# A tiled 4096 x 4096 x 4096 matmul with bias and tanh: the opening's loads of B moved to SyncE as float32, A put first on GpSimd's queue, the first phase cut from eight k-tiles to six, and transposes moved ahead of adds

## The chip, the cores and the metric

The kernel runs on one core of a Trainium2 chip. The metric is the device time of one execution in microseconds (us), lower is better. Rates: 1 GB/s is 1 KB/us, and 1 MB/us is 1,000 of these. A load "lands" when its last byte has arrived.

## The reference

```python
def setup_inputs():
    m, k, n = 4096, 4096, 4096
    return {"a": randn(m, k), "b": randn(k, n), "bias": randn(n)}    # float32

def reference(a, b, bias):
    return np.tanh(np.matmul(a, b) + bias)
```

## The kernel before

The kernel multiplies in float16, with A's contraction index k on the partitions. A k-tile is a group of 128 values of k. GpSimd's loads cast from float32 to float16 on the way in; VectorE (DVE) turns A in 32 x 32 blocks. The partitions are used as four quarters of 32: partition 32q + p of k-tile t holds row 1024q + 32t + p of B. So one k-tile of B is four separate strips of 32 rows, each loaded by a DMA of its own.

The steady state (most of the run) multiplies rows of A, 128 at a time, with a 1024-column strip of B that lies in SBUF. The opening is special, because B's first strip has to arrive first. It works on two groups of four row tiles, in this order: group 0 on the first `KS` k-tiles, group 1 on the same `KS` k-tiles, then group 0 on the rest, then group 1 on the rest. The kernel has eight PSUM buffers, so partial sums are put aside in SBUF (`spill`) and added later.

```python
    KS = 8                       # k-tiles in the first phase (of KT = 32)
    AN = 3                       # buffers for untransposed A
    WARM = 24                    # matmuls on zeros, to warm the clock
    ...
    def load_b(bt, n0, t0, nt, q):               # one of four quarters, cast by GpSimd's DMA
        src = b[ds(q * KQ + t0 * QP, nt * QP), ds(n0, NCW)]
        nc.gpsimd.dma_start(out=bt[t0 // TB][ds(q * QP, QP), ds(t0 % TB, nt), :],
                            in_=src.rearrange("(t p) n -> p t n", p=QP))
    ...
    def turn(at, key, mb0, t0, nt):              # transpose on VectorE, frees A's buffer after use
        pump()                                   # issues queued loads, at most AN of A
        transpose_a(at, staged[key][0], mb0, t0, nt)
        ...
    want_a("g0a", 2, 0, 2 * Q, 0, KS)            # the queue of loads, all on GpSimd
    want(lambda: load_b_all(0, 2))
    want_a("g0b", 2, 2 * P, 2 * Q, 0, KS)
    for t in range(2, KS, 2):
        want(lambda t=t: load_b_all(t, 2))
    want(lambda: load_bias(bias_bc, 0))
    want_a("g1a", 2, 4 * P, 2 * Q, 0, KS)
    want_a("g1b", 2, 6 * P, 2 * Q, 0, KS)
    for t in range(KS, KT, TA):                  # TA = 8: then A and B for the rest
        want_a(("g0", t), G, 0, G * Q, t, TA)
        for u in range(t, t + TA, TB):
            want(lambda u=u: load_b_all(u, TB))
    for m in range(G):
        want_a(("g1", m), 1, (G + m) * P, Q, KS, KT - KS)
    ...
    def aside0(ps, m, j):                        # group 0's first sums are put aside ...
        put_aside(ps, m, j)
        if (m, j) == (1, 1):
            turn1(0)                             # ... group 1's first transpose among them
    down(ps, KS - 2, KS, aside0)
    turn1(1)
    ...
    def end0(ps, m, j):                          # group 0's last adds, tanh and stores
        end(ps, m, j)
        if (m, j) == (1, 1):
            turn2(0)                             # group 1's next transpose, behind four adds
    down(ps, KT - TB, KT, end0)
```

Of the kernel before, what the change touches and what calls it, by code (L numbers as in the profile page):

```python
# [13 lines left out]
P = 128  # L14
Q = 4
QP = 32
NB = 512
fp32 = mybir.dt.float32
# [4 lines left out]
def kernel(  # L23
# [7 lines left out]
    nc = tc.nc  # L31
# [4 lines left out]
    KQ = K // Q  # L36
    KT = K // P
    MT = M // P
    NCW = 1024
    NC = N // NCW  # L40
    J = NCW // NB
    TB = 4
    G = 4
    KS = 8
    AN = 3
    WARM = 24

    singles = ctx.enter_context(tc.tile_pool(name="singles", bufs=1))
    bpool = ctx.enter_context(tc.tile_pool(name="bpool", bufs=2))
# [2 lines left out]
    biasp = ctx.enter_context(tc.tile_pool(name="biasp", bufs=2))  # L52
# [32 lines left out]
            an[:, ds(mb0, Q), :].rearrange("P mb (t k) -> P mb t k", k=QP),  # L85
        )

    def load_bias(bias_bc, n0):
        src = bias[ds(n0, NCW)]
        nc.gpsimd.dma_start(  # L90
            out=bias_bc,
            in_=bass.AP(tensor=src.tensor, offset=src.offset, ap=[[0, P], *src.ap]),
        )


    queue, live, staged = [], [0], {}
# [9 lines left out]
    def want_a(key, uses, *where):  # L106
        queue.append((key, uses, lambda: load_a(*where)))

    def want(load):
        queue.append((None, 0, load))  # L110

    def turn(at, key, mb0, t0, nt):
        pump()
        transpose_a(at, staged[key][0], mb0, t0, nt)
        staged[key][1] -= 1
        if not staged[key][1]:
            live[0] -= 1
            pump()
# [3 lines left out]
            ps, at[:, t, :], bt[t // TB][:, t % TB, ts(j, NB)], start=start, stop=stop  # L122
        )

    def finish(ps, addend, mi, c0, w=NB, o_sb=None, pieces=1):

        if o_sb is None:
            o_sb = opool.tile([P, w], fp32, name="o_sb")
        w //= pieces
        for i in range(pieces):  # L130
            piece = ds(i * w, w)
            nc.vector.tensor_tensor(  # L132
                out=o_sb[:, piece], in0=ps[:, piece], in1=addend[:, piece], op=mybir.AluOpType.add
            )
            nc.scalar.activation(  # L135
                o_sb[:, piece], o_sb[:, piece], mybir.ActivationFunctionType.Tanh
            )
            nc.sync.dma_start(out=out[ds(mi * P, P), ds(c0 + i * w, w)], in_=o_sb[:, piece])



# [12 lines left out]
    def put_aside(ps, m, j):  # L154
        nc.vector.tensor_tensor(  # L155
            out=aside(m, j), in0=ps, in1=bias_bc[:, ts(j, NB)], op=mybir.AluOpType.add
        )

    def end(ps, m, j):
        finish(ps, aside(m, j), m, j * NB, o_sb=aside(m, j))  # L160

    def banks():
        return [[psum.tile([P, NB], fp32, name="ps") for j in range(J)] for m in range(G)]

    def load_b_all(t0, nt):
        for q in range(Q):
            load_b(b_cur, 0, t0, nt, q)

    def across(ps, ms, t0, nt, first):
        for t in range(t0, t0 + nt):  # L170
            for m in ms:
                for j in range(J):
                    mm(ps[m][j], ats[m], b_cur, t, j, t == first, False)

    def down(ps, t0, t1, done):
        for m in range(G):
            for j in range(J):
                for t in range(t0, t1):
                    mm(ps[m][j], ats[m], b_cur, t, j, False, t == t1 - 1)
                done(ps[m][j], m, j)  # L180
# [15 lines left out]
        nc.tensor.matmul(warm, zeros[:, :P], zeros, start=i == 0, stop=i == WARM - 1)  # L196


    TA = 8
    want_a("g0a", 2, 0, 2 * Q, 0, KS)  # L200
    want(lambda: load_b_all(0, 2))
    want_a("g0b", 2, 2 * P, 2 * Q, 0, KS)
    for t in range(2, KS, 2):
        want(lambda t=t: load_b_all(t, 2))
    bias_bc = biasp.tile([P, NCW], fp32, name="bias_bc")
    want(lambda: load_bias(bias_bc, 0))
    want_a("g1a", 2, 4 * P, 2 * Q, 0, KS)
    want_a("g1b", 2, 6 * P, 2 * Q, 0, KS)
    for t in range(KS, KT, TA):
        want_a(("g0", t), G, 0, G * Q, t, TA)  # L210
        for u in range(t, t + TA, TB):
            want(lambda u=u: load_b_all(u, TB))
    for m in range(G):
        want_a(("g1", m), 1, (G + m) * P, Q, KS, KT - KS)
    todo = [(c, mi) for c in range(NC) for mi in range(MT) if (c, mi) >= (0, 2 * G)]

    ps = banks()
    turn(ats[0], "g0a", 0, 0, KS)
    turn(ats[1], "g0a", Q, 0, KS)
    across(ps, (0, 1), 0, 2, 0)  # L220
    turn(ats[2], "g0b", 0, 0, KS)
    turn(ats[3], "g0b", Q, 0, KS)
    across(ps, (2, 3), 0, 2, 0)
    across(ps, range(G), 2, KS - 4, 0)

    def turn1(m):
        turn(ats[G + m], "g1a" if m < 2 else "g1b", (m % 2) * Q, 0, KS)

    def aside0(ps, m, j):
        put_aside(ps, m, j)  # L230
        if (m, j) == (1, 1):
            turn1(0)

    down(ps, KS - 2, KS, aside0)
    turn1(1)


    def turn0(t, m):
        turn(ats[m], ("g0", t), m * Q, t, TA)

    def before1(m, j):
        if m < 6 and j == 0:
            turn1(m - 2)
        if m == 6:
            turn0(KS, j)
        if m == 7:
            turn0(KS, 2 + j)

    group1(0, KS, put_aside, before1)


    ps = banks()
    for t in range(KS, KT, TA):
        if t > KS:
            for m in range(G):
                turn0(t, m)
        across(ps, range(G), t, TA - TB if t + TA == KT else TA, KS)

    def turn2(m):
        turn(ats[G + m], ("g1", m), 0, KS, KT - KS)  # L260

    def end0(ps, m, j):
        end(ps, m, j)
        if (m, j) == (1, 1):
            turn2(0)

    down(ps, KT - TB, KT, end0)


    ahead = 3  # L270
# [24 lines left out]
    for i, (c, mi) in enumerate(todo):  # L295
        if mi == 0:
            b_cur, bias_bc = b_next, bias_next
        if c + 1 < NC and mi == (2 * G if c == 0 else 0):
            b_next = new_b()
            left = [(s, q) for s in range(KT // TB) for q in range(Q)]  # L300
        if i + ahead < len(todo):
            want_row(i + ahead)
        for s, q in left[:2]:
            want(lambda s=s, q=q, c=c, bt=b_next: load_b(bt, (c + 1) * NCW, s * TB, TB, q))
        left = left[2:]
        if c + 1 < NC and mi == MT - 4:
            bias_next = biasp.tile([P, NCW], fp32, name="bias_bc")
            want(lambda c=c, bb=bias_next: load_bias(bb, (c + 1) * NCW))
        pump()
        if i + 2 < len(todo):  # L310
            new_at(i + 2)
        at = at_q.pop(0)
        for j in range(J):

            halves = 2 if i == len(todo) - 1 and j == J - 1 else 1
            w = NB // halves
            for h in range(halves):
                ps = psum.tile([P, w], fp32, name="ps")
                c0 = j * NB + h * w
                for t in range(KT):  # L320
                    nc.tensor.matmul(  # L321
                        ps,
                        at[:, t, :],
                        b_cur[t // TB][:, t % TB, ds(c0, w)],
                        start=t == 0,
                        stop=t == KT - 1,
                    )
                finish(ps, bias_bc[:, ds(c0, w)], mi, c * NCW + c0, w, pieces=halves)


# [28 lines left out]
```

## Time and profile before

| | before |
|---|---|
| time, median of the first 3 runs | 1792.26 us (1791.81 to 1792.65) |
| matmuls of the product | 8,192 of 0.2158 us = 1,768 us |
| first matmul of the product starts | 11.35 us |
| last matmul ends, span ends | 1785.5 us, 1789.8 us |
| B's k-tiles 24 to 27 land, first used | 70.8 us, 71.6 us |
| group 1's second block of A lands, its transpose starts | 79.6 us, 82.8 us |

The page of before opens with the busy time of each engine, in us, and its share of the span; its clock row has one digit for each fortieth of the span.

```profile
PE 1779.1 (99%) x8248; PEld 807.4 (45%) x8248; DVE 745.0 (42%) x420; ACT 162.7 (9%) x260; POOL 358.0 (20%) x668
...
PEclk9999999999999999999999999999999999999999
```

TensorE is busy 99% of the span at full clock, on this scale. All there is to win is in the first 90 us and the last 4, so the views below look at those. First, TensorE's waits in before: who ended them, us in total, how many, the longest.

```profile
PE ps L121 <- DMA b<-in_b_dram: 2.9, 1, 2.9
PE ps L121 <- DVE atx L83: 1.3, 2, 0.7
...
PE ps L121 <- DVE at L83: 1.0, 1, 1.0
```

The 2.9 us are the wait for B at 8.5 to 11.35 us. The 1.0 us is for the second block of A. The 1.3 us are two waits for group 1's transposes, 0.7 us near 29 us and 0.62 us near 86 us.

Next, stretches of before: us from the span's start, length, then busy us and instructions of PE, PEld, DVE, ACT and POOL, the granted clock, the DMA share and the GB/s written by DMAs.

```profile
5.00:10.00 5.00, 3.45 (x16) 1.40 (x14) 2.17 (x2) 0.00 (x0) 3.63 (x7) 1.00 1.08 143
10.00:15.00 5.00, 3.05 (x8) 0.93 (x8) 1.14 (x2) 0.00 (x0) 3.81 (x8) 0.69 1.28 195
15.00:20.00 5.00, 4.55 (x14) 1.54 (x15) 1.42 (x2) 0.00 (x0) 4.25 (x8) 0.63 1.11 197
40.00:50.00 10.00, 10.00 (x48) 4.51 (x47) 5.10 (x6) 0.00 (x0) 4.45 (x8) 1.00 1.30 202
```

The clock is the share of full speed that TensorE was granted, a mean over the stretch. It is 0.69 and 0.63 between 10 and 20 us, after TensorE had nothing to do from 8.5 to 11.35 us. The DMAs write float16, so 202 GB/s written are about 0.40 MB/us read. The first ten microseconds are far below that.

Last, the timeline of before: start, length, engine, line, operation, how many, and in brackets the idle time ahead of it and what ended that.

```profile
11.35 3.05 PE L121 MATMUL ps<-b,at 128*128 128x512 f16 x8 [2.90 <-DMA b<-in_b_dram]
...
14.05 2.37 DVE L83 STREAM_TRANSPOSE at<-an 128x1024 f16<-128x1024 f16 x2 [3.86 <-DMA an<-in_a_dram]
...
15.36 14.06 PE L121 MATMUL ps<-b,at 128*128 128x512 f16 x56 [0.95 <-DVE at L83]
...
82.80 3.37 DVE L83 STREAM_TRANSPOSE atx<-an 128x3072 f16<-128x3072 f16 x1
...
86.23 9.02 PE L121 MATMUL ps<-b,atx 128*128 128x512 f16 x41 [0.62 <-DVE atx L83]
```

The transposes for rows 2 and 3 start at 14.05 us and the matmuls that need them at 15.36. (K-tile 24's first use, 71.6 us in the table, is group 0's second phase at 44.0 us plus 128 matmuls of 0.2158 us; no wait lies between.) At 82.80 us group 1's transpose starts although its data landed at 79.6 us: it stands behind group 0's adds in VectorE's order, and TensorE waits for it until 86.23 us.

### The profile page before, as it was taken

The page shows a single profiled execution, that of the slowest core. Times are in us where ns is not written, and L with a number is a line of the kernel's source. Part 1 is how long each engine was busy: PE and PEld are TensorE (multiplying, and loading weights), DVE is VectorE, ACT ScalarE, POOL GpSimd, SP SyncE. Part 2 cuts the span into 40 slices and gives each one's busy share as a digit, 9 for nine tenths or more (in the row PEclk, how much of TensorE's full clock was granted, in tenths as well). Part 3 has the DMA queues.
Part 4 walks back from the last instruction along what each step waited for, and adds up shares of the span by engine and source line. Part 5 has one row for each costly group of instructions (what it writes and reads, how often), then busy time and mean ns, then how long its engine had stood idle before and what let it go on. Part 6 is the DMA issues. An engine that isn't in the chain of part 4 may idle for free.

```text
span 1789.8 us, 19352 instructions
## 1 busy us (share of the span) xinstructions
PE 1779.1 (99%) x8248; PEld 807.4 (45%) x8248; DVE 745.0 (42%) x420; ACT 162.7 (9%) x260; POOL 358.0 (20%) x668
## 2 busy tenths in 40 slices
PE   8999999999999999999999999999999999999999
PEld 3444444444444444444444444444444444444444
DVE  5463344334433444334433443344334433444341
ACT  0110000000000000000000000000000000000001
POOL 6422222211222211111132222111111111111100
PEclk9999999999999999999999999999999999999999
DMA  9999887665777865655588777555665555655621
GB/s 182 214 189 189 155 159 147 125 132 114 159 147 144 170 140 108 121 119 124 106 168 156 158 142 142 121 112 107 127 120 112 112 113 109 125 112 111 120 70 41
DMA packets 138630, 238.26 MB, mean 133 GB/s; under 512 B 14769, under 2 KB 27569, under 8 KB 138545
## 3 DMA queue, kind: packets, MB, share of 16 engines
q0 software_dynamic: 101248, 169.91, 56.6%
q1 hardware_dynamic: 37296, 67.13, 10.3%
q8 instruction: 64, 1.05, 0.2%
q14 instruction: 22, 0.17, 0.0%
HBM read 337.64 MB, written 67.11 MB: 226 GB/s over the span
## 4 chain that ended last, share of the span: by engine, by line
PE 95%; DMA 4%; POOL 1%; issue 1%; DVE 0%; ACT 0%; ACTq 0%; DVEq 0%; POOLq 0%
PE ps L321 92%; PE ps L121 2%; DMA b<-in_b_dram 2%; DMA an<-in_a_dram 1%; POOL b L66 0%; DMA bias_bc<-in_bias_dram 0%; POOL an L75 0%; DVE atx L83 0%; ACT o_sb L135 0%; DVE o_sb L132 0%; ACTq L354 0%; DVEq L132 0%; POOLq L343 0%
## 5 line engine op out<-in xcount | busy, mean ns | idle before, releaser
L321 PE MATMUL ps<-b,at 128*128 128x512 f16 x7712 | 1657.8, 378 | 0.0
L321 PEld LDWEIGHTS <-at 128*128 128x128 f16 x7712 | 754.6, 98 | 903.3
L132 DVE TENSOR_TENSOR o_sb<-ps,bias_bc 128x512 f32<-128x512 f32 (+1 forms) x243 | 166.4, 686 | 977.8 <-PE ps L321 764.1
L83 DVE STREAM_TRANSPOSE at<-an 128x4096 f16<-128x4096 f16 (+1 forms) x136 | 551.0, 4056 | 26.7 <-DMA an<-in_a_dram 26.7
L75 POOL DMA_DIRECT2D an<-in_a_dram x524 | 282.8, 547 | 1296.6 <-DVE at L83 1224.4
L135 ACT ACTIVATE o_sb<-o_sb 128x512 f32<-128x512 f32 (+1 forms) x243 | 151.5, 624 | 1505.7 <-DVE o_sb L132 1505.7
L66 POOL DMA_DIRECT2D b<-in_b_dram x136 | 73.2, 542 | 55.2 <-PE ps L321 28.6
L121 PE MATMUL ps<-b,at 128*128 128x512 f16 x256 | 58.6, 391 | 3.9 <-DMA b<-in_b_dram 2.9
L121 PE MATMUL ps<-b,atx 128*128 128x512 f16 x256 | 55.7, 379 | 1.3 <-DVE atx L83 1.3
L121 PEld LDWEIGHTS <-at 128*128 128x128 f16 x256 | 25.3, 100 | 37.1 <-issue 5.7
L121 PEld LDWEIGHTS <-atx 128*128 128x128 f16 x256 | 24.8, 98 | 32.2 <-DVE atx L83 2.7
L132 DVE TENSOR_TENSOR spill<-ps,spill 128x512 f32<-128x512 f32 x16 | 10.7, 684 | 25.7 <-PE ps L121 25.4
L135 ACT ACTIVATE spill<-spill 128x512 f32<-128x512 f32 x16 | 10.0, 630 | 117.2 <-DVE spill L132 117.2
L83 DVE STREAM_TRANSPOSE atx<-an 128x1024 f16<-128x1024 f16 (+1 forms) x8 | 18.3, 2295 | 0.0
L155 DVE TENSOR_TENSOR spill<-ps,bias_bc 128x512 f32<-128x512 f32 x16 | 10.1, 670 | 10.0 <-PE ps L121 10.0
L196 PE MATMUL ps<-zeros 128*128 128x512 f16 x24 | 7.3, 476 | 1.2 <-DVE zeros L193 1.2
L196 PEld LDWEIGHTS <-zeros 128*128 128x128 f16 x24 | 2.8, 118 | 5.2 <-issue 2.5
L90 POOL DMA_DIRECT2D bias_bc<-in_bias_dram x4 | 2.3, 563 | 0.1
L135 ACT ACT_TABLE_LOAD x1 | 1.3, 1283 | 0.7 <-PEq L343 0.7
L193 DVE MEMSET zeros<- 128x256 uint32 x1 | 0.3, 272 | 0.9 <-PEq L343 0.9
L343 POOL MEMSET const-float32-0.0<- 128x1 f32 x1 | 0.1, 98 | 0.2 <-issue 0.2
L343 POOL MEMSET const-bfloat16-1.0<- 128x1 bf16 x1 | 0.1, 101 | 0.0
(2 smaller groups left out, 0.2 us busy)
## 6 DMA issues: line engine op xcount, KB each, us to landing
an<-in_a_dram POOLq DMA_DIRECT2D x492, 256.0 KB, 5.4
out_dram<-o_sb SPq DMA_DIRECT2D x239, 256.0 KB, 4.3
b<-in_b_dram POOLq DMA_DIRECT2D x120, 256.0 KB, 8.9
out_dram<-spill SPq DMA_DIRECT2D x16, 256.0 KB, 6.4
an<-in_a_dram POOLq DMA_DIRECT2D x16, 192.0 KB, 7.8
an<-in_a_dram POOLq DMA_DIRECT2D x16, 128.0 KB, 5.7
b<-in_b_dram POOLq DMA_DIRECT2D x16, 128.0 KB, 5.0
bias_bc<-in_bias_dram POOLq DMA_DIRECT2D x4, 512.0 KB, 8.2
```

The source lines that it names most:

```text
L66: nc.gpsimd.dma_start(out=bt[t0 // TB][ds(q * QP, QP), ds(t0 % TB, nt), :], in_=src.rearrange("(t p) n -> p t n", p=QP),)
L75: nc.gpsimd.dma_start(out=an[ds(q * QP, QP), :, :], in_=src.rearrange("(mb p) k -> p mb k", p=QP),)
L83: nc.vector.transpose(at[:, ds(t0, nt), :].rearrange("P t (mb p) -> P mb t p", p=QP), an[:, ds(mb0, Q), :].rearrange("P mb (t k) -> P mb t ...
L90: nc.gpsimd.dma_start(out=bias_bc, in_=bass.AP(tensor=src.tensor, offset=src.offset, ap=[[0, P], *src.ap]),)
L121: nc.tensor.matmul(ps, at[:, t, :], bt[t // TB][:, t % TB, ts(j, NB)], start=start, stop=stop)
L132: nc.vector.tensor_tensor(out=o_sb[:, piece], in0=ps[:, piece], in1=addend[:, piece], op=mybir.AluOpType.add)
L135: nc.scalar.activation(o_sb[:, piece], o_sb[:, piece], mybir.ActivationFunctionType.Tanh)
L155: nc.vector.tensor_tensor(out=aside(m, j), in0=ps, in1=bias_bc[:, ts(j, NB)], op=mybir.AluOpType.add)
L193: nc.vector.memset(zeros, 0.0)
L196: nc.tensor.matmul(warm, zeros[:, :P], zeros, start=i == 0, stop=i == WARM - 1)
L321: nc.tensor.matmul(ps, at[:, t, :], b_cur[t // TB][:, t % TB, ds(c0, w)], start=t == 0, stop=t == KT - 1,)
L343: nc = _bacc.Bacc("TRN2", target_bir_lowering=False, num_devices=1)
```

## The change

The intent is to start the product earlier and to keep the clock up. B's first six k-tiles come over SyncE's queue as float32, which needs no cast, and ScalarE, idle in the opening, rounds them to float16. GpSimd's queue then starts with A alone. The first phase shrinks from eight k-tiles to six. Group 1's transposes move ahead of group 0's adds in two places. The bias moves to SyncE too, and the very last store goes out on ScalarE's queue.

```diff
-    KS = 8
+    KS = 6
-    WARM = 24
+    WARM = 18
@@ the queue of loads
     want_a("g0a", 2, 0, 2 * Q, 0, KS)
-    want(lambda: load_b_all(0, 2))
     want_a("g0b", 2, 2 * P, 2 * Q, 0, KS)
-    for t in range(2, KS, 2):
-        want(lambda t=t: load_b_all(t, 2))
-    want(lambda: load_bias(bias_bc, 0))
     want_a("g1a", 2, 4 * P, 2 * Q, 0, KS)
     want_a("g1b", 2, 6 * P, 2 * Q, 0, KS)
-    for t in range(KS, KT, TA):
-        ... A and B for eight k-tiles at a time
+    SA = [(KS, 6), (12, 6), (18, 7), (25, 7)]
+    SB = [[(6, 2), (8, 4)], [(12, 4)], [(16, 4), (20, 4)], [(24, 4), (28, 4)]]
+    ... A and B by SA and SB
+    def raw_b(t):
+        return spill[3 - t // 2].rearrange("P (h x) n -> P h (x n)", h=2)[:, t % 2, :]
+    for t in range(KS):
+        for q in range(Q):
+            nc.sync.dma_start(out=raw_b(t)[ds(q * QP, QP), :],
+                              in_=b[ds(q * KQ + t * QP, QP), ds(0, NCW)])
+    load_bias(bias_bc, 0, nc.sync)
+    for t in range(KS):
+        nc.scalar.copy(b_cur[t // TB][:, t % TB, :], raw_b(t))
@@ the transposes
-    down(ps, KS - 2, KS, aside0)      # turn1(0) after the fourth add
+    turn1(0)
+    down(ps, KS - 2, KS, put_aside)
-    down(ps, KT - TB, KT, end0)       # turn2(0) after the fourth add
+    turn2(0)
+    down(ps, KT - TB, KT, end)
@@ the last two stores
-                finish(..., pieces=halves)
+                queues = (nc.sync, nc.scalar) if halves > 1 else (nc.sync,)
+                finish(..., queues=queues)
```

More of the change, by code (lines that the diff above doesn't have):

```diff
@@ L86, in transpose_a, with load_bias @@
         )
-    def load_bias(bias_bc, n0):
+    def load_bias(bias_bc, n0, queue):
         src = bias[ds(n0, NCW)]
-        nc.gpsimd.dma_start(
+        queue.dma_start(
             out=bias_bc,
@@ L123, in mm, with finish @@
         )
-    def finish(ps, addend, mi, c0, w=NB, o_sb=None, pieces=1):
+    def finish(ps, addend, mi, c0, w=NB, o_sb=None, queues=(nc.sync,)):
         if o_sb is None:
             o_sb = opool.tile([P, w], fp32, name="o_sb")
-        w //= pieces
-        for i in range(pieces):
+        w //= len(queues)
+        for i, queue in enumerate(queues):
             piece = ds(i * w, w)
@@ L137, in finish @@
             )
-            nc.sync.dma_start(out=out[ds(mi * P, P), ds(c0 + i * w, w)], in_=o_sb[:, piece])
+            queue.dma_start(out=out[ds(mi * P, P), ds(c0 + i * w, w)], in_=o_sb[:, piece])
     b_cur = new_b()
@@ L196 @@
         nc.tensor.matmul(warm, zeros[:, :P], zeros, start=i == 0, stop=i == WARM - 1)
-    TA = 8
     want_a("g0a", 2, 0, 2 * Q, 0, KS)
-    want(lambda: load_b_all(0, 2))
     want_a("g0b", 2, 2 * P, 2 * Q, 0, KS)
-    for t in range(2, KS, 2):
-        want(lambda t=t: load_b_all(t, 2))
-    bias_bc = biasp.tile([P, NCW], fp32, name="bias_bc")
-    want(lambda: load_bias(bias_bc, 0))
     want_a("g1a", 2, 4 * P, 2 * Q, 0, KS)
     want_a("g1b", 2, 6 * P, 2 * Q, 0, KS)
-    for t in range(KS, KT, TA):
-        want_a(("g0", t), G, 0, G * Q, t, TA)
-        for u in range(t, t + TA, TB):
-            want(lambda u=u: load_b_all(u, TB))
+    SA = [(KS, 6), (12, 6), (18, 7), (25, 7)]
+    SB = [[(6, 2), (8, 4)], [(12, 4)], [(16, 4), (20, 4)], [(24, 4), (28, 4)]]
+    for (t, nt), bs in zip(SA, SB):
+        want_a(("g0", t), G, 0, G * Q, t, nt)
+        for u, nu in bs:
+            want(lambda u=u, nu=nu: load_b_all(u, nu))
     for m in range(G):
@@ L215 @@
     todo = [(c, mi) for c in range(NC) for mi in range(MT) if (c, mi) >= (0, 2 * G)]
+    def raw_b(t):
+        return spill[3 - t // 2].rearrange("P (h x) n -> P h (x n)", h=2)[:, t % 2, :]
+    for t in range(KS):
+        for q in range(Q):
+            nc.sync.dma_start(
+                out=raw_b(t)[ds(q * QP, QP), :],
+                in_=b[ds(q * KQ + t * QP, QP), ds(0, NCW)],
+            )
+    bias_bc = biasp.tile([P, NCW], fp32, name="bias_bc")
+    load_bias(bias_bc, 0, nc.sync)
+    for t in range(KS):
+        nc.scalar.copy(b_cur[t // TB][:, t % TB, :], raw_b(t))
     ps = banks()
-    turn(ats[0], "g0a", 0, 0, KS)
-    turn(ats[1], "g0a", Q, 0, KS)
+    for m in range(2):
+        turn(ats[m], "g0a", m * Q, 0, KS)
     across(ps, (0, 1), 0, 2, 0)
-    turn(ats[2], "g0b", 0, 0, KS)
-    turn(ats[3], "g0b", Q, 0, KS)
+    for m in range(2):
+        turn(ats[2 + m], "g0b", m * Q, 0, KS)
     across(ps, (2, 3), 0, 2, 0)
@@ L227, in turn1, with turn0 @@
         turn(ats[G + m], "g1a" if m < 2 else "g1b", (m % 2) * Q, 0, KS)
-    def aside0(ps, m, j):
-        put_aside(ps, m, j)
-        if (m, j) == (1, 1):
-            turn1(0)
-    down(ps, KS - 2, KS, aside0)
+    turn1(0)
+    down(ps, KS - 2, KS, put_aside)
     turn1(1)
-    def turn0(t, m):
-        turn(ats[m], ("g0", t), m * Q, t, TA)
+    def turn0(i, m):
+        turn(ats[m], ("g0", SA[i][0]), m * Q, *SA[i])
     def before1(m, j):
@@ L244, in before1 @@
         if m == 6:
-            turn0(KS, j)
+            turn0(0, j)
         if m == 7:
-            turn0(KS, 2 + j)
+            turn0(0, 2 + j)
     group1(0, KS, put_aside, before1)
     ps = banks()
-    for t in range(KS, KT, TA):
-        if t > KS:
+    for i, (t, nt) in enumerate(SA):
+        if i:
             for m in range(G):
-                turn0(t, m)
-        across(ps, range(G), t, TA - TB if t + TA == KT else TA, KS)
+                turn0(i, m)
+        across(ps, range(G), t, min(t + nt, KT - TB) - t, KS)
     def turn2(m):
         turn(ats[G + m], ("g1", m), 0, KS, KT - KS)
-    def end0(ps, m, j):
-        end(ps, m, j)
-        if (m, j) == (1, 1):
-            turn2(0)
-    down(ps, KT - TB, KT, end0)
+    turn2(0)
+    down(ps, KT - TB, KT, end)
     ahead = 3
@@ L307 @@
             bias_next = biasp.tile([P, NCW], fp32, name="bias_bc")
-            want(lambda c=c, bb=bias_next: load_bias(bb, (c + 1) * NCW))
+            want(lambda c=c, bb=bias_next: load_bias(bb, (c + 1) * NCW, nc.gpsimd))
         pump()
@@ L327 @@
                     )
-                finish(ps, bias_bc[:, ds(c0, w)], mi, c * NCW + c0, w, pieces=halves)
+                queues = (nc.sync, nc.scalar) if halves > 1 else (nc.sync,)
+                finish(ps, bias_bc[:, ds(c0, w)], mi, c * NCW + c0, w, queues=queues)
 _INS = ['a', 'b', 'bias']
```

## The prediction

> **What bounds the kernel now.** TensorE is busy 99% of the span (the page's first part). 8,192 matmuls at 0.2158 us (chain of waits) need 1,768 us. The other 22 us: first real matmul at 11.35 us (timeline); about 3 us of cold clock (granted 0.69 and 0.63 in the windows from 10 to 20 us); three later waits, 2.3 us; 4.3 us after the last matmul.
>
> Behind TensorE, loads bound the first 80 us: the windows show about 205 GB/s written as float16, so 0.41 MB/us of float32 read. By its landing, B's k-tiles 24 to 27 arrive at 70.8 us, 0.8 us before use. Group 1's next block of A lands at 79.6 us; its transpose starts at 82.8, behind group 0's adds, hence a 0.62 us wait at 86 us.
>
> **What the change does.**
> 1. Start. B comes over SyncE, past GpSimd's issues (0.53 us each, eight in flight). Six ScalarE copies: from the tanh of 512 (0.63 us) and 128 (about 0.3 us) columns I estimate 1.05 us each. First real matmul: 8 to 11 us, central 9.
> 2. Clock. Warm-up ends near 7 us; little cold stretch follows. Steps 1, 2 and the gaps: up to 8 us.
> 3. Loads. The Trainium skill, "DMA: Bandwidth & Descriptors", section "Issuing engines are not separate DMA queues": all engines' DMAs share the same 16 DMA engines; only issue time is saved. So the later rate does not rise. Gained is the slow start (71 to 180 KB/us written until 12 us), 2.5 to 3 us of DMA time, and 0.5 MB less A is read before k-tile 24 (1.3 us). A's rows shrink from 1 KB to 768 or 896 bytes (minus 0.5 us).
> 4. KS 8 to 6. The first phase (both groups on the same k-tiles) shortens: 16 matmuls (3.45 us) less are done before the loads' deadlines.
> 5. Transposing group 1 first removes the 0.62 us wait if its load is in time; otherwise the adds wait too.
> 6. The last store on ScalarE's queue: 0.3 us.
>
> **On the critical path.** Adding up the queue's bytes at rates that reproduce before's landings to 0.4 us, k-tiles 24 to 27 land near 67 us; TensorE, unhindered from 9 us, wants them at 61. So it runs into the loads: waits of 2 to 3 us near k-tiles 12 and 16, 1 us near 24, perhaps one at group 1's transpose. Group 1's second pass starts at 81 us instead of 86.2, with 16 more matmuls left: 5.2 - 3.45 = 1.7 us gained, plus 0.3 at the end.
>
> **Prediction: 1790.0 us, 8 in 10 between 1786.5 and 1793.0.** Faster by over 2%: 0.005; within 2%: 0.99; slower by over 2%: 0.005.
>
> **What would show it.** Right: first real matmul by 11 us, clock warm through 20 us; TensorE waits for loads of 4 to 8 us between 30 and 82 us; DMA at 200 to 210 KB/us (float16) from 20 to 75 us; k-tiles 24 to 27 landing at 66 to 68 us; group 1's second pass at 80 to 82 us. Wrong: no waits after the opening and a gain of 6 us or more.
>
> **What would make it wrong.** Two queues together moving more than one: 1784 to 1786. A's 768-byte rows costing far more than 1 KB rows: 1794 or more. A wait near k-tile 16 cooling the clock: 2 us slower.

## The result, and the profile after

The changed kernel took 1793.23 us (median of 4 runs, 1793.06 to 1793.6), before 1792.03 us (4 runs, 1791.03 to 1792.65). The ratio is 1.0008, with a 95% interval from 0.999 to 1.0025. The time is within 2% of before's, as predicted. But 1793.2 lies just above the stated range, 3.2 us above the number given, and no gain shows at all.

| | before | after |
|---|---|---|
| A's first block lands (four loads) | 7.7 us | 9.9 us |
| first matmul of the product | 11.35 us | 11.06 us |
| read from HBM by 10, 16, 30 us | 1.98, 4.33, 9.67 MB | 2.31, 4.26, 9.16 MB |
| B's k-tiles 24 to 27 land | 70.8 us | 70.6 us |
| matmuls done when k-tile 24 starts | 256 | 240 |
| last matmul ends | 1785.5 us | 1787.25 us |
| from there to the end of the span | 4.3 us | 3.7 us |

(The bytes read are summed from the DMA packet records: float16 written counts double, float32 and the bias once. Landings are from the same trace's completion records.)

TensorE's waits in the changed kernel:

```profile
PE ps L121 <- DVE at L83: 7.1, 3, 4.4
...
PE ps L121 <- DMA b<-in_b_dram: 0.3, 1, 0.3
PE ps L121 <- DVE atx L83: 0.2, 1, 0.2
PE ps L121 <- DVE spill L155: 0.2, 1, 0.2
```

The waits for A's transposes grew from 1.0 to 7.1 us (4.4 us ahead of the first matmul, 2.5 us ahead of rows 2 and 3). Of the waits for loads that the prediction placed at k-tiles 12 to 24, 0.3 us is left.

Stretches of the changed kernel, with the columns as before:

```profile
5.00:10.00 5.00, 1.71 (x8) 0.59 (x6) 0.00 (x0) 2.71 (x3) 2.70 (x5) 1.00 1.24 228
10.00:15.00 5.00, 3.54 (x8) 0.86 (x8) 1.84 (x2) 1.71 (x2) 1.72 (x3) 0.66 1.26 242
15.00:20.00 5.00, 2.63 (x7) 0.85 (x8) 1.84 (x2) 1.64 (x2) 2.22 (x4) 0.78 1.29 245
40.00:50.00 10.00, 9.72 (x46) 4.35 (x46) 4.19 (x6) 0.00 (x0) 4.77 (x9) 1.00 1.30 202
```

The clock is as cold as before. From 5 to 20 us the DMAs write 228 to 245 GB/s, which looks like more than before's 143 to 197. But B is now written as float32, so each byte written is only one byte read, and read bytes are what the opening needs.

The timeline of the changed kernel, in the lines that answer to those of before:

```profile
7.67 1.04 ACT L226 CAST b<-spill 128x1024 f16<-128x1024 f32 x1
...
10.03 1.84 DVE L83 STREAM_TRANSPOSE at<-an 128x768 f16<-128x768 f16 x2 [8.89 <-DMA an<-in_a_dram]
...
11.06 3.54 PE L121 MATMUL ps<-b,at 128*128 128x512 f16 x8 [4.36 <-DVE at L83]
...
16.08 1.84 DVE L83 STREAM_TRANSPOSE at<-an 128x768 f16<-128x768 f16 x2 [4.21 <-DMA an<-in_a_dram]
...
17.97 9.97 PE L121 MATMUL ps<-b,at 128*128 128x512 f16 x38 [0.25 <-DVE at L83]
...
70.71 13.97 PE L121 MATMUL ps<-b,at 128*128 128x512 f16 x64 [0.29 <-DMA b<-in_b_dram]
...
79.82 3.65 DVE L83 STREAM_TRANSPOSE atx<-an 128x3328 f16<-128x3328 f16 x1 [10.04 <-DMA an<-in_a_dram]
...
84.52 10.74 PE L121 MATMUL ps<-b,atx 128*128 128x512 f16 x49
```

ScalarE has rounded B's first k-tile by 8.7 us, and then A is what is missing: it is transposed from 10.03 us for rows 0 and 1 and from 16.08 us for rows 2 and 3. The k-tile 24 starts at 70.71 us, a moment after its B has landed. Group 1's transpose at 79.82 us now stands ahead of the adds, and no wait precedes the matmuls of group 1.

The account closes. Before starts k-tile 24 at 71.6 us with 256 matmuls done and waits another 0.62 us later. After starts it at 70.7 us with 240 done. So the last matmul should end 70.7 - 71.6 + 16 x 0.2158 - 0.62 = 1.9 us later; the trace has 1.73. The tail gives back 0.6 us. The difference of the medians is 1.2 us.

### The profile page after: what moved, and what is told of

Read it like the earlier page. It is cut to its first block, busy times and chain, and to the rows that moved or that the text cites. A ratio compares the mean times of both kernels' runs of the same rounds, so it can differ in the third digit from the quotient of the medians.

```text
span 1791.0 us, 19389 instructions
## 1 busy us (share of the span) xinstructions
PE 1778.1 (99%) x8242; PEld 806.7 (45%) x8242; DVE 745.2 (42%) x424; ACT 168.8 (9%) x266; POOL 354.8 (20%) x659
## 3 DMA queue, kind: packets, MB, share of 16 engines
q8 instruction: 64, 1.05, 0.2%
## 4 chain that ended last, share of the span: by engine, by line
PE 96%; DMA 3%; POOL 0%; issue 0%; DVE 0%; ACT 0%; DVEq 0%; POOLq 0%
PE ps L324 92%; PE ps L121 4%; DMA an<-in_a_dram 2%; DMA b<-in_b_dram 1%; POOL an L75 0%; DVE at L83 0%; DVE spill L155 0%; ACT o_sb L135 0%; DVE atx L83 0%; DVE o_sb L132 0%; DVEq L83 0%; DVEq L132 0%; DVEq L155 0%; POOLq L347 0%
## 5 line engine op out<-in xcount | busy, mean ns | idle before, releaser
L83 DVE STREAM_TRANSPOSE at<-an 128x4096 f16<-128x4096 f16 (+2 forms) x140 | 551.4, 3944 | 30.5 <-DMA an<-in_a_dram 30.5
L66 POOL DMA_DIRECT2D b<-in_b_dram x124 | 67.0, 544 | 46.6 <-PE ps L324 28.6
L121 PEld LDWEIGHTS <-at 128*128 128x128 f16 x256 | 25.1, 100 | 42.1 <-DVE at L83 10.3
L83 DVE STREAM_TRANSPOSE atx<-an 128x768 f16<-128x768 f16 (+1 forms) x8 | 18.3, 2297 | 14.3 <-DMA an<-in_a_dram 14.3
L226 ACT CAST b<-spill 128x1024 f16<-128x1024 f32 x6 | 6.3, 1045 | 9.2 <-DMA spill<-in_b_dram 9.2
```

What stands on the lines that cost most here:

```text
L83: nc.vector.transpose(at[:, ds(t0, nt), :].rearrange("P t (mb p) -> P mb t p", p=QP), an[:, ds(mb0, Q), :].rearrange("P mb (t k) -> P mb t ...
L121: nc.tensor.matmul(ps, at[:, t, :], bt[t // TB][:, t % TB, ts(j, NB)], start=start, stop=stop)
L226: nc.scalar.copy(b_cur[t // TB][:, t % TB, :], raw_b(t))
```

## The experiments

The theory that came out of this comparison (L) is that the loads set the pace until about 71 us: what counts is when B's k-tile 24 lands and how much work is done by then. The rival (C) is that the change lost its gain in its opening, to the late block of A and the cold clock. A second question stood behind L: why did B's loads, freed from GpSimd's issues, land no earlier?

### 1. The changed kernel with the clock held up (e1_warm)

```diff
-    WARM = 18
+    WARM = 38
@@ between rows 0, 1 and rows 2, 3
+    for i in range(20):
+        nc.tensor.matmul(ps[2][0], zeros[:, :P], zeros, start=i == 0, stop=i == 19)
```

> The changed kernel with the clock held up: 38 warm-up matmuls for 18, and 20 more on zeros in the wait ahead of rows 2 and 3. Theory L (until 71 us the loads set the pace, and B's k-tiles 24 to 27 land no earlier whatever TensorE does): the cold stretch goes, TensorE arrives earlier at k-tile 24 and waits there 2 to 4 us for B instead of 0.3; time within 0.5 us of the changed kernel, so 1 to 1.5 us above before. Rival C (the change lost its gain to the starved first block of A and the cold clock): about 3 us less than the changed kernel, so about 2 us below before.

Measured: 1793.82 us (5 runs), before 1791.52, ratio 1.0013 (1.0000 to 1.0026). The clock stayed at full speed from 4.7 us on, and nothing was gained. TensorE's waits in this run:

```profile
PE ps L122 <- DVE atx L84: 1.8, 1, 1.8
...
PE ps L122 <- DMA b<-in_b_dram: 0.5, 1, 0.5
...
```

The microseconds won by the clock came back as waits: 1.8 us for group 1's second transpose, until 30.9 us, and 0.5 us for B at k-tile 24, which started at 71.1 us (70.7 in the changed kernel). As far as the clock goes, rival C falls: its 3 us did not come. The late block of A stayed (first matmul at 11.1 us), so that half of C is not tested by this run. The wait appeared mostly at another place than expected, but it is again a load that sets it: group 0's adds, which stand ahead of that transpose, waited 2.0 us for the bias, the last load in SyncE's queue, until 25.1 us.

### 2. Before with six k-tiles in the first phase, nothing else (e2_ks6)

```diff
-    KS = 8
+    KS = 6
-    (A in chunks of 8 k-tiles from k-tile 8)
+    (A in chunks of 6, 6, 7, 7 k-tiles from k-tile 6, as in the change)
```

> Before with a first phase of six k-tiles instead of eight, all else as before (B cast by GpSimd's loads, same order, same warm-up). Theory L: 16 matmuls (3.45 us) less are done before the loads' deadline at k-tile 24, whose bytes come 1.3 us earlier; 0.8 us of slack is used up, so 1 to 2 us slower than before, with a new wait for B near k-tile 24. Rival C: the size of the first phase does not matter, within 0.5 us of before.

Measured: 1795.91 us (5 runs), before 1791.52, ratio 1.0026 (1.0012 to 1.0039): 4.4 us slower, more than expected. TensorE's part of this run's timeline, from the start of group 0's second phase:

```profile
37.62 9.01 PE L121 MATMUL ps<-b,at 128*128 128x512 f16 x41 [0.18 <-DVE spill L155]
47.32 7.07 PE L121 MATMUL ps<-b,at 128*128 128x512 f16 x32 [0.69 <-DMA b<-in_b_dram]
57.08 13.97 PE L121 MATMUL ps<-b,at 128*128 128x512 f16 x64 [2.69 <-DMA b<-in_b_dram]
71.95 13.97 PE L121 MATMUL ps<-b,at 128*128 128x512 f16 x64 [0.89 <-DMA b<-in_b_dram]
86.80 5.57 PE L121 MATMUL ps<-b,atx 128*128 128x512 f16 x25 [0.89 <-DVE atx L83]
```

The idle times in brackets are new waits for B: 0.69 us at k-tile 12, 2.69 at 16, 0.89 at 24, and 0.89 for the transpose that follows. This is the pattern that the prediction had put into the changed kernel. The smaller first phase costs 4.4 us when it stands alone; the changed kernel, with the rest of the change, is 1.2 us slower than before.

Why more than expected? The expectation had the bytes for k-tile 24 come 1.3 us earlier. They came 1.0 us later: B's k-tiles 24 to 27 land at 71.8 us (70.8 in before). By 30 us 8.87 MB had been read (9.67 in before, 9.16 in the changed kernel). So the smaller first phase puts the loads 0.8 MB behind without a single float32 load. Two stretches of this run, in which only A is loaded, and one of the changed kernel, where A is alone too:

```profile
22.00:24.00 2.00, 1.60 (x8) 0.52 (x6) 2.00 (x4) 0.00 (x0) 2.00 (x4) 1.00 1.48 169
24.00:26.00 2.00, 1.54 (x8) 0.72 (x9) 2.00 (x4) 0.00 (x0) 2.00 (x4) 1.00 1.40 161
```

```profile
24.00:26.00 2.00, 2.00 (x11) 0.88 (x9) 1.04 (x2) 0.00 (x0) 1.98 (x4) 1.00 1.59 189
```

The last figure of each is the GB/s written. GpSimd issues nearly all the time in all three, and the rows are the same; why the loads are slower in this run is not shown.

### 3. B's float32 loads with nothing beside them (e3_b_alone)

```diff
     def load_a(...):
         an = anat.tile(...)
+        if hold:                       # the first three loads of A wait for the last k-tile of B
+            nc.scalar.copy(an[:, 0, :QP], raw_b(KS - 1)[:, :QP])
```

> A measurement, slow on purpose: the changed kernel with A's first three loads held until B's six float32 k-tiles have landed and been copied, so SyncE's loads run alone. If mixing with A's small rows or with GpSimd's queue costs rate, B alone lands 3.1 MB at 0.38 to 0.41 MB/us, in about 8 us, all by 11 us. If the form of B's loads (128 KB each, float32 written to 32 partitions) is the slow part, it takes 10 us or more (0.31 MB/us or less).

Measured (one look, 1802.04 us, slow on purpose): the last of the 24 loads landed at 16.55 us. In the steady part one load of 131 KB landed every 0.55 us, which is 0.24 MB/us. That is the second alternative, and below its 0.31 MB/us: B's float32 loads alone ran at little more than half of the 0.41 MB/us that casting loads reach. So they are slow without A and without a second queue beside them.

### 4. The changed kernel with eight k-tiles in the first phase (e4_ks8)

```diff
-    KS = 6
+    KS = 8
```

> The changed kernel with a first phase of eight k-tiles (eight float32 k-tiles of B by SyncE, A's rows 1 KB again). Theory L: 3.45 us more work done ahead of the deadlines; loads land at about the same time as before, so 0.5 to 2 us below before (the order of the transposes and the tail store remain gained). Rival C: A still starved by B (first block of A landing at 10 us or later) and the cold clock remain, so as slow as the changed kernel, 1 us above before.

Measured: 1794.23 us (5 runs), before 1791.52, ratio 1.0015 (1.0002 to 1.0027). The expectation of L was missed: it is no faster than the changed kernel. With eight k-tiles of float32 the opening is so late that it, not k-tile 24, sets the time: first matmul at 12.1 us, a wait of 3.5 us ahead of rows 2 and 3, the last float32 k-tile landing at 29.1 us, and no wait for a load after that. Read by 30 us: 8.55 MB, against 9.67 in before, and B's k-tiles 24 to 27 land at 73.7 us, 2.9 us later than in before, which has the same size of first phase. So with eight k-tiles the move of B to SyncE as float32 does not bring the loads forward; it puts them back. (The new order does not do it: in experiment 6 they land at 70.9 us.) That a larger first phase would help with faster loads is not shown (experiment 8). (The change may have gone to six k-tiles for this reason; no run shows the intent.)

### 5. Seven forms of the same load, each by itself (f4_forms)

Ahead of the kernel before, 3.1 MB of B were loaded seven times, each series starting after the one before it had landed.

```diff
+    # 1: SyncE, float32, 32 partitions x 4 KB, 128 KB a load (as in the change)
+    # 2: SyncE, the same, two k-tiles a load, 256 KB
+    # 3: SyncE, 128 partitions x 4 KB, 512 KB a load
+    # 4: as 1, SyncE and ScalarE in turn
+    # 5: GpSimd, float32 without cast, 32 partitions, 256 KB a load
+    # 6: SyncE, 128 partitions x 1 KB, 128 KB a load
+    # 7: GpSimd, cast to float16, 32 partitions, two k-tiles a load (as before)
```

> A measurement: before, with seven series of loads ahead of it, one after the other, each of the same 3.1 MB of float32 from B. (1) as in the change, SyncE, 32 partitions of 4 KB, 128 KB each: 0.24 MB/us as in the run with B alone. (2) the same with two k-tiles a load, 256 KB: if a fixed cost per load is the cause, 0.30 MB/us or more; if the write of float32 to 32 partitions is, 0.24 again. (3) 128 partitions of 4 KB, 512 KB each: 0.38 or more either way. (4) as 1 but SyncE and ScalarE in turn: 0.30 or more if the fixed cost is one queue's; 0.24 if not. (5) GpSimd, float32 without cast, 256 KB: as 2 if the write is the cause, 0.38 or more if SyncE's path is. (6) SyncE, 128 partitions of 1 KB, 128 KB each: 0.24 if the load's size is the cause, 0.35 or more if the 32 partitions are. (7) GpSimd casting to float16, 32 partitions, as before: 0.39 to 0.42.

Measured (one look, all 1900.82 us of it on purpose). One window inside each series, in this order; the last column is the GB/s written.

```profile
5.00:12.00 7.00, 3.99 (x16) 1.52 (x14) 0.00 (x0) 0.00 (x0) 0.00 (x0) 1.00 1.04 234
24.00:32.00 8.00, 0.00 (x0) 0.00 (x0) 0.00 (x0) 0.00 (x0) 0.00 (x0) 0.50 1.04 221
42.00:48.00 6.00, 0.00 (x0) 0.00 (x0) 0.00 (x0) 0.00 (x0) 0.00 (x0) 0.50 0.96 335
56.00:64.00 8.00, 0.00 (x0) 0.00 (x0) 0.00 (x0) 0.00 (x0) 0.00 (x0) 0.50 1.04 241
75.00:84.00 9.00, 0.00 (x0) 0.00 (x0) 0.00 (x0) 0.00 (x0) 1.19 (x3) 0.50 1.04 222
91.00:99.00 8.00, 0.00 (x0) 0.00 (x0) 0.00 (x0) 0.00 (x0) 0.00 (x0) 0.50 0.84 248
108.00:114.00 6.00, 0.00 (x0) 0.00 (x0) 0.00 (x0) 0.00 (x0) 4.99 (x10) 0.50 1.09 183
```

The forms 1, 2, 4 and 5 write 221 to 241 GB/s: twice the load's size, a second queue, or GpSimd in place of SyncE change little. Form 3, the same float32 to 128 partitions, writes 335 GB/s in a window with one gap of 3.1 us between landings; its other landings are 1.22 to 1.34 us apart, or about 0.41 MB/us. Form 7 writes only 183 GB/s in its window but reads twice that, and in its steady part lands a load of 262 KB read every 0.63 us, 0.41 MB/us. So the slow form is float32 written to 32 partitions at a time. A casting load to the same 32 partitions writes half the bytes for the same bytes read, and comes out at the full rate. Form 6 can't tell its two cases apart: SyncE issued a load every 0.47 us, so that its 248 GB/s are near the 0.28 MB/us that the issues allow. No run here shows why 32 partitions are slower.

### 6. The order of the transposes and the last store alone (f1_order_tail)

```diff
-    down(ps, KS - 2, KS, aside0)      # before
+    turn1(0)
+    down(ps, KS - 2, KS, put_aside)
-    down(ps, KT - TB, KT, end0)
+    turn2(0)
+    down(ps, KT - TB, KT, end)
+    (the last piece's store on ScalarE's queue)
```

> Before with only two parts of the change: group 1's transposes ahead of group 0's adds, and the last piece's store on ScalarE's queue. Expected: the 0.62 us wait near 86 us and most of the 0.71 us wait near 29 us go; the first only counts if B's k-tile 24 is not waited for (0.8 us of slack), so TensorE ends 0.6 to 1.3 us earlier, and the tail shortens from 4.3 to about 3.8 us: 1 to 1.8 us below before. If these parts cost something, it is not below before.

Measured: 1791.00 us (5 runs), before 1791.68, ratio 0.9996 (0.9982 to 1.0009): 0.7 us less, inside the noise of the times, and less than the 1 to 1.8 us expected. The trace says more: group 1's transpose starts at 79.7 us and the wait near 86 us is gone, but the wait near 29 us moved and grew, from 0.7 to 1.2 us. In the earlier place all eight of group 0's adds now stand between group 1's first and second transpose. The tail is 4.1 us instead of 4.3. The later of the two moves pays, the earlier one doesn't.

### 7. That kernel with the clock held up (f2_warm)

```diff
-    WARM = 24
+    WARM = 38        # and 10 matmuls on zeros ahead of rows 2 and 3
```

> The previous kernel (order and tail) with the clock held through the opening: 38 warm-up matmuls for 24 and 10 more ahead of rows 2 and 3. Theory L: TensorE comes about 3 us earlier to k-tile 24 and waits there for B, which lands at the same time (70.8 us): only 0.8 us or less of the 3 us shows, the rest is a new wait of about 2 us at k-tile 24. Rival C: all 3 us show.

Measured: 1790.48 us (5 runs), before 1791.68, ratio 0.9994 (0.9982 to 1.0007). Little of the 3 us shows, as L says (the last matmul ends 0.4 us earlier than in experiment 6), but the new wait did not come at k-tile 24: it is 1.7 us at group 1's second transpose (1.2 in the kernel of experiment 6). Group 1's first transpose, now ahead of the adds, started when its block of A had landed at 26.1 us; the eight adds followed, and the second transpose started only at 32.2 us.

### 8. That kernel with ten k-tiles in the first phase (f3_ks10)

```diff
-    KS = 8
+    KS = 10          # B still cast by GpSimd's loads; WARM = 42, 12 more ahead of rows 2 and 3
```

> The previous kernel (order, tail, warm clock) with a first phase of ten k-tiles, B still cast by GpSimd's loads. Theory L: 3.45 us more work is done before the deadlines, so the wait at k-tile 24 shrinks to under 1 us and most of the held clock's 3 us shows, less about 1 us for the longer first load of A: 2.5 to 4.5 us below before. If the size of the first phase is not what counts: no better than the previous kernel.

Measured: 1791.09 us (5 runs), before 1791.68, ratio 0.9998 (0.9986 to 1.0011). The expectation of 2.5 to 4.5 us below before was missed. No wait for a load is left, but the larger first block of A delays the first matmul to 12.8 us, and 1.1 us are lost at the same transpose. With ten k-tiles the later start costs what the later slack wins; B's k-tiles 24 to 27 land at 71.4 us and are first used at 75.5.

### 9. Float32 B to 128 partitions (g1_wide)

```diff
-        for q in range(Q):
-            nc.sync.dma_start(out=raw_b(t)[ds(q * QP, QP), :],
-                              in_=b[ds(q * KQ + t * QP, QP), ds(0, NCW)])
+        nc.sync.dma_start(out=raw_b(t), in_=b[ds(t * P, P), ds(0, NCW)])
```

The result is wrong (128 consecutive rows are not the right ones).

> The changed kernel with one difference: each float32 k-tile of B comes as one load of 128 consecutive rows to 128 partitions (512 KB) instead of four of 32 partitions. The rows are not the right ones, so the result is wrong on purpose; bytes, queue, copies and order are the same. If the mis-sized term is the rate of float32 written to 32 partitions (0.23 MB/us alone, against 0.41 to 128): B's six k-tiles land by 14 to 17 us instead of 22, B's k-tiles 24 to 27 by 66.5 to 68.5 us instead of 70.6, and the time falls to 1789.5 to 1791.5 us, with waits for loads near k-tiles 12 to 24: the prediction, once its rate holds. If the mixing of two queues or A's small rows is the cause, k-tiles 24 to 27 still land at 70 us or later and the time stays within 0.5 us of the changed kernel.

Measured: 1792.83 us (5 runs), before 1791.97, ratio 1.0003 (0.9990 to 1.0015). Stretches of this run, columns as before, and TensorE's wait for A:

```profile
5.00:10.00 5.00, 2.42 (x10) 0.89 (x8) 0.00 (x0) 2.87 (x4) 1.56 (x3) 1.00 1.14 337
10.00:15.00 5.00, 0.00 (x0) 0.00 (x0) 0.28 (x1) 2.71 (x3) 1.26 (x3) 0.74 1.26 303
15.00:20.00 5.00, 4.24 (x12) 1.46 (x13) 4.38 (x5) 0.00 (x0) 3.60 (x7) 0.57 1.44 164
20.00:25.00 5.00, 5.00 (x25) 2.25 (x23) 0.00 (x0) 0.00 (x0) 4.38 (x8) 1.00 1.31 146
```

```profile
PE ps L121 <- DVE at L83: 8.3, 1, 8.3
```

Up to 15 us the DMAs write 303 to 337 GB/s, nearly all of it float32. Read by 16 us: 5.21 MB, against 4.26 in the changed kernel. That lead of 0.95 MB is 2.4 us of DMA time at 0.40 MB/us, about what the prediction had counted on, and B's six k-tiles are all there at 12.8 us. But B's wide loads crowd out A's: from 4 to 12 us A is written at only 29 to 40 KB/us (70 to 80 in the changed kernel, whose loads of B have rows of 4 KB too, so the length of the rows alone does not explain it). A's first block is complete at 14.6 us, and TensorE waits 8.3 us. From 15 to 25 us only 146 to 164 GB/s are written. A's buffers were freed late and GpSimd issued A's loads of 96 KB no faster than one in 0.57 us; both fit, and neither is tested alone. In experiment 2 the first block came at 6.8 us, and its loads still fell 0.5 MB further behind before's between 16 and 30 us; here 0.7 MB of the lead over before went. Of the lead, B's k-tiles 24 to 27 keep 1.1 us: they land at 69.4 us, not at 66.5 to 68.5 as expected. The time is then set by the late start, not by the loads: no wait stands at k-tile 24, and the last matmul ends 0.4 us earlier than in the changed kernel. The expectation was missed in both numbers: the right rate is not enough.

### 10. The same in 1 KB pieces (h1_wide_1k)

```diff
+        for c in range(4):
+            nc.sync.dma_start(out=raw_b(t)[:, ds(c * 256, 256)],
+                              in_=b[ds(t * P, P), ds(c * 256, 256)])      # wrong rows, on purpose
```

> The changed kernel with B's float32 k-tiles in loads of 128 partitions by 1 KB of a row (24 loads of 128 KB, wrong rows on purpose), so that B neither is written slowly (as with 32 partitions) nor crowds out A's 768-byte rows (as the 4 KB rows of the run to 128 partitions did: A's first block at 14.6 us). If those two are what the prediction missed, all of it holds here: A's first block by 9 us, first real matmul by 10.5, B's k-tiles 24 to 27 at 66.5 to 68.5 us, waits of several us for loads between 30 and 72 us, time 1789 to 1791 us. If something else is the cause, k-tiles 24 to 27 stay past 69 us and the time within 0.7 us of the changed kernel.

Measured: 1792.37 us (5 runs), before 1791.70, ratio 1.0006 (0.9993 to 1.0020). A's first block lands at 9.5 us and the first matmul starts at 10.6. But with 24 loads of 128 KB the slow start is back: 4.33 MB read by 16 us, as before the change. SyncE issues one in 0.47 us at first, which may be the cause; no run separates it. B's k-tiles 24 to 27 land at 70.1 us, and TensorE waits 0.8 us for them. The expectation was missed, but the time follows the landing: 0.5 us earlier at k-tile 24 than the changed kernel, and the last matmul ends 0.5 us earlier.

### 11. 128 partitions and A first (h2_a_first)

```diff
+    load_raw(0)                                  # k-tile 0 at once, 512 KB, wrong rows on purpose
+    turn(ats[0], "g0a", 0, 0, KS)
+    (VectorE marks k-tiles 1 to 5, then SyncE loads them and the bias)
+    turn(ats[1], "g0a", Q, 0, KS)
```

> The run with 512 KB loads to 128 partitions (wrong rows on purpose), but B's k-tiles 1 to 5 and the bias are loaded only after A's first block has been transposed, so that they can't crowd it out. In that run 5.2 MB had been read by 16 us (4.3 in the changed kernel, 4.3 in before), and the lead was lost from 16 to 24 us, where A's loads waited for buffers that the late first block had not freed. Here A's first block lands by 7 us and the lead should be kept: at least 9.9 MB read by 30 us (9.2 in the changed kernel), B's k-tiles 24 to 27 by 67 to 69 us, first real matmul by 10 us, waits for loads of 2 to 6 us between 30 and 72 us, time 1789 to 1791.3 us. If k-tiles 24 to 27 land past 69.5 us again, the lead is lost to something not named yet.

Measured: 1792.49 us (5 runs), before 1791.93, ratio 1.0000 (0.9987 to 1.0014). A's first block landed at 7.6 us and the first matmul started at 8.8 us, the earliest of all runs. Read by 30 us: 9.79 MB, just under the 9.9 expected. Then B's k-tile 1 came only at 15.3 us, and TensorE waited 6.2 us for it. The late adds (from 25.7 us, behind the wait) freed group 1's buffer of A late, and from 34 to 38 us the rate fell to 156 to 172 KB/us written. B's k-tiles 24 to 27 landed at 69.8 us, past the 69.5 that the expectation set as its limit. By its own terms, then, the lead was lost to something not named beforehand; in this trace a held buffer fits, and no run tests that by itself.

### 12. The right rows to 128 partitions (h4_wide_right2)

```diff
+                in_=b[:, ds(c * 256, 256)].rearrange("(q r) n -> q r n", q=Q)[:, ds(t * QP, QP), :]
```

> As the run with 1 KB pieces to 128 partitions, with the right rows of B (source in four groups of 32 rows). If the loads use all 16 DMA engines like the others, it gives the same time with a correct result. If the grouping of the source keeps them from that, or the rows land elsewhere, it is slower or wrong, and shows only that.

Measured: correct, 1834.34 us (4 runs), before 1791.70, ratio 1.0240 (1.0226 to 1.0254): 42 us slower. In the first 20 us all DMAs together wrote 106 GB/s. The Trainium skill, "DMA: Bandwidth & Descriptors", section "Why a DMA increments its semaphore by 16 and not by 1", says that a DMA runs on the largest number of engines up to 16 that divides the slowest dimension of both access patterns; worked out from this, an estimate, a source in four groups gets four. This run agrees in direction (TensorE waits 42.4 us in all for the copies of B) and doesn't show the number. With the k order that this kernel gives to its partitions, the wide form was not to be had cheaply.

### 13. Before with the parts that pay (g2_lace, g3_bias_early, g4_b0_raw)

```diff
 g2_lace: clock held up, last store on ScalarE's queue, turn2(0) ahead of the adds, and
+        if (m, j) == (0, 1): turn1(0)           # group 1's first two transposes between the adds
+        if (m, j) == (2, 1): turn1(1)
 g3_bias_early: g2_lace, and
-    want(lambda: load_bias(bias_bc, 0))         # GpSimd, after B's first eight k-tiles
+    load_bias(bias_bc, 0, nc.sync)              # SyncE, first of all
 g4_b0_raw: g3_bias_early, and B's k-tile 0 alone as float32 by SyncE, copied by ScalarE
            (the bias behind its four loads; 34 warm-up matmuls instead of 38)
```

> The kernel with order, tail store and held clock, but group 1's first two transposes laced between group 0's adds (after the second and the sixth) instead of the first ahead of all eight and the second behind them; the later one (near 80 us) stays ahead. The 1.65 us wait for the second transpose near 32 us should go; then TensorE reaches k-tile 24 about 0.6 us before B lands (70.4 us). 1 us less than that kernel's 1790.5 if the loads allow it: 1 to 2.5 us below before.

> As the one before, with the bias loaded first thing over SyncE (the change's own idea, alone): its 1.3 us of DMA time falls where the DMA engines are not yet full. Theory L: B's k-tiles 24 to 27 land 0.7 to 1.3 us earlier (69 to 69.8 us) and no wait for them is left, 0 to 0.7 us below the one before.

> As the one before, with B's first k-tile alone as float32 over SyncE and copied by ScalarE (4 loads instead of the change's 24), the rest cast by GpSimd's loads. First real matmul at about 10 us instead of 11.4; loads 0.5 us earlier or the same, so TensorE waits 0.5 to 1 us more for them: 0 to 0.8 us below the one before.

Measured, 5 runs each on one chip, before 1791.97 us: g2_lace 1789.76 (ratio 0.9986, 0.9973 to 1.0000), g3_bias_early 1789.39 (0.9984, 0.9971 to 0.9996), g4_b0_raw 1790.95 (0.9992, 0.9980 to 1.0005).

TensorE's waits in g3_bias_early, the first line of the view (for the zeros) left out:

```profile
...
PE ps L122 <- DVE at L84: 0.5, 1, 0.5
PE ps L122 <- DVE spill L156: 0.2, 1, 0.2
```

These 0.7 us are all the waits, and the clock stays up. The bias, sent over SyncE at 0.75 us and landed at 5.1, uses time in which the DMA engines have little to do (in before the DMA share is 0.53 until 5 us, and 1.08 from 5 to 10): 10.31 MB are read by 30 us instead of 9.73 in g2_lace (9.67 in before), the most of all kernels here, and B's k-tiles 24 to 27 land at 69.0 us, as expected. Of the two steps, the difference of 0.4 us between g2_lace and g3_bias_early is too small for the times to show. g2_lace, whose loads come no earlier (70.7 us), gains what order and clock can: k-tile 24 starts at 70.7 us (71.6 in before), after 0.4 us of waiting for B, its only wait for a load, and the 0.6 us near 86 us are gone. g4_b0_raw missed: four of the change's 24 float32 loads already delay A's first block from 8.4 to 10.2 us and bring the bytes read by 30 us down to 9.15 MB, and the kernel is 1.6 us slower than g3_bias_early on the same chip. The kernel g3_bias_early beats before with an interval that excludes 1. It is also below the changed kernel, which was not in the same rounds: its ratio to before is 0.9984 (0.9971 to 0.9996), the changed kernel's 1.0008 (0.9990 to 1.0025), so those two intervals overlap and the times alone do not settle it.

## Why the prediction was wrong

The prediction named the right stage and the right limit. The step that failed is its step 3, the sum of the loads: two of its terms were mis-sized, so that k-tiles 24 to 27 landed at 70.6 us and not near 67; the time missed by 3.2 us.

- **Right: the loads take back what TensorE wins early.** The prediction said that TensorE would run into the loads. Experiment 1 shows it for the clock: with it full from 4.7 us, the changed kernel is not faster.
- **Right in direction: the smaller first phase costs.** Step 4 put 3.45 us on it, less what step 3 saved in bytes; alone it costs 4.4 us (experiment 2), with waits of 0.7, 2.7 and 0.9 us at k-tiles 12, 16 and 24, where the prediction had 2 to 3, 2 to 3 and 1.
- **Right: the later order and the tail.** The wait near 86 us is gone. The tail is 0.6 us shorter, against 0.3 predicted; in experiment 6, which has the same last store, it is 0.25 shorter, and experiment 2, which has not, also has 0.3, so that the store's share is not settled.
- **Right: the later load rate.** From 40 to 50 us it is 202 GB/s in both kernels.
- **Right: the copy.** The six copies take 1.04 us each, estimated at 1.05. The Trainium skill, "ScalarE: Activation LUTs", section "What ACT_TABLE_LOAD costs", gives 186 ns + 0.833 ns per element for an ACTIVATE with immediate scale and bias. Worked out for 1,024 elements this is an estimate of 1.04 us; the trace, which calls these copies CAST, agrees.
- **Wrong, and the step that failed: step 3's "Gained is the slow start (71 to 180 KB/us written until 12 us), 2.5 to 3 us of DMA time".** The loads did not get ahead. By 30 us 9.16 MB had been read instead of 9.67, so the loads were 0.5 MB or about 1.2 us behind before (at 0.41 MB/us) instead of 2.5 to 3 us ahead. With 0.5 MB less to read before k-tile 24, the landing came out nearly even, 0.2 us earlier than in before. The sum had given float32 loads the rate of casting loads, about 0.4 MB/us. Measured by themselves, float32 rows written to 32 partitions run at 0.22 to 0.24 MB/us (experiments 3 and 5). With a wide form in their place, a lead of 2.4 us over the changed kernel appears by 16 us (experiment 9). So the slow form is shown to cost that lead. Of B's landing the wide form brings 1.1 us, and of the time nothing clear.
- **Wrong, in the same step: "0.5 MB less A is read before k-tile 24 (1.3 us). A's rows shrink from 1 KB to 768 or 896 bytes (minus 0.5 us)".** This would have B's k-tiles 24 to 27 land 0.8 us earlier. With the smaller first phase alone, and B still cast by GpSimd, they land 1.0 us later, and 0.8 MB less has been read by 30 us (experiment 2). That is 1.8 us of the 3.6 by which the landing missed 67 us. From experiment 2 to the changed kernel the landing gains 1.2 us, where 2.5 to 3 were counted on: the other half. The halves depend on the order in which one adds the parts: with eight k-tiles, float32 over SyncE does not gain 1.2 us but comes with a landing 2.9 us later (experiment 4).
- **Wrong: the start.** Central 9 us, measured 11.06 us, just outside the stated 8 to 11. A's first block landed at 9.9 us instead of 7.7. Where B's loads run at full rate, it comes at 14.6 us (experiment 9). The prediction did not see this. That the late start cost nothing by itself in the changed kernel is argued from the wait for B at k-tile 24; no run moves the start alone. The danger that it did name, A's 768-byte rows costing far more than 1 KB rows, is not excluded: alone, from 24 to 26 us, they are written at 189 KB/us in the changed kernel, near before's 1 KB rows at 193, but at 161 to 169 from 22 to 26 us in experiment 2.
- **Wrong: the clock.** "Little cold stretch follows" failed: 0.66 and 0.78 from 10 to 20 us, since TensorE waited 4.4 and 2.5 us for A. This cost nothing by itself (experiment 1).
- **Wrong: the waits and the second pass.** It had waits for loads of 4 to 8 us between 30 and 82 us; the trace has 0.3 us for B. TensorE came to k-tile 24 late enough that loads and work met there. Group 1's second pass started at 84.5 us, not at 81.

**Open.** No run brought k-tiles 24 to 27 to the predicted 67 us with this order of loads. Each cure of the slow form lost part of the lead again (experiments 9 to 11), and the reasons given there, A crowded out, buffers freed late, many small issues, are argued from traces. All of these kernels have the smaller first phase, which loses 0.5 MB between 16 and 30 us by itself (experiment 2). So two things are shown: the slow form costs the lead by 16 us, and the smaller first phase costs landing time instead of saving it. Why the smaller first phase slows the loads is not settled.

## What to carry to other kernels

When a stage is bound by loads, count what arrives by the deadline, not when the first work starts: in the changed kernel a warm clock was worth nothing, and with before's loads (g2_lace) no more than the 0.9 us by which k-tile 24 could start earlier. A DMA rate belongs to a form (here the type written and the number of partitions made the difference), so a load moved to another queue and another type has to be measured in its new form before it enters a sum. Making loads fewer or smaller is such a new form too: 0.5 MB less to read came 1.0 us later here. And two queues may share the DMA engines unevenly (33 KB/us for A beside 314 for B in experiment 9), so that the load wanted first may be the one that is starved.

## What the Trainium skill lacked or had wrong

- "DMA: Bandwidth & Descriptors": no rate for loads that cast on the way. Here a casting load to 32 partitions read 0.41 MB/us of float32, where float32 written to 32 partitions without a cast ran at 0.22 to 0.24 MB/us, whatever the queue or the size of the load (experiment 5).
- The same page, section "Issuing engines are not separate DMA queues", held: SyncE and ScalarE in turn wrote 241 GB/s, SyncE alone 234. The page has no measured shares of a GpSimd load and a SyncE load that run together: here, beside wide loads of B at about 315 KB/us, A's 768-byte rows were written at 29 to 40 KB/us, and its first block came at 14.6 us instead of 7.7.
- The same page, section "Anatomy of one DMA", puts descriptor generation at "small, variable", without a time there. Here each of GpSimd's loads keeps it for 0.53 to 0.70 us (0.57 for most of A's loads of 96 KB), so loads of 96 KB written can't be issued faster than 0.34 MB/us read, below the 0.41 that larger ones reach. That this time is all descriptor generation is not shown.
